# Branch projections in seven block products for two output tiles, with the weights' sums and parts made earlier and kept in DRAM

## The chip, the cores and the metric

The kernel runs on one core of one Trainium2 chip. The metric is device time in microseconds (us) of one execution. The time before is the median of three runs. Rows of the trace come from one profiled execution.

## The reference

One layer of a decoder: a normalized input, one input projection, three branches with gates, a projection of each branch, a merge by sigmoid gates, an output projection. Cut to what is computed around the change:

```python
mod = jax.nn.silu(c) @ w_ada + b_ada
shift, scale, gate = jnp.split(mod[:, None, :], 3, axis=-1)
h = _rmsnorm(x, norm_g) * (1 + scale) + shift
p = h @ w_in
a_b, a_c, a_h, a_g, b_u, b_v, b_g, c_x, c_g, m_a, m_b, m_c = jnp.split(p, IN_SPLITS, axis=-1)
...
merged = (jax.nn.sigmoid(m_a) * (y_a @ w_branch[0])
          + jax.nn.sigmoid(m_b) * (y_b @ w_branch[1])
          + jax.nn.sigmoid(m_c) * (y_c @ w_branch[2]))
x = x + gate * (merged @ w_out)
```

There are 1024 prompt positions and 8 samples, so T = 1032 columns, in two halves of H = 516 or four quarters of HC = 258. The model's width is 1024; `y_a`, `y_b`, `y_c` are 512 wide, so `w_branch` is three matrices of 512 x 1024. Everything is float32.

## The kernel before

Activations lie with features on partitions and positions on columns. A float32 product is made of three: each operand is split into a high part (a copy that rounds, on ScalarE) and a low part (a subtraction, on VectorE; both in `split`, L94 to L96), and TensorE forms high x high, high x low and low x high.

The stages, in order of time. **Head** (to about 30 us): x is loaded in eight tiles, ScalarE squares them, VectorE adds most squares (L206, L214), TensorE sums the rest over the partitions (`sum_squares`, `ss`, L190), then come the reciprocal root (`rm0x` and on), its spread over partitions (`spx` from `dgx`) and the modulation (`pada`). `warm_up` issues fill matmuls on a constant (`warm`, L308). **v stage** (30 to 88). **Input projection** (88 to 669): 28 pairs of output tiles, each by `pair_jobs` as seven block products of 24 matmuls of 258 columns in place of eight (Strassen's scheme). **Merge** (669 to 811): `merge_jobs` for the branches 1, 0, 2; for each of eight output tiles `wjob` issues 36 matmuls of 344 columns (four row blocks, three chunks, three parts) from one weight `p_...` and the branch output `yh`, `yl`, then VectorE multiplies by the gate `sig` (L1010, L1013) and adds to `acc` (L1014). **Output projection** (811 to 918).

From the projection on the work is a list of jobs. Each has a `dma`, a `split`, an `mm` and a `post`. `run_ahead` issues a job's `dma` and `split` so many us before its `mm` by the sum of the planned durations (`ahead`); `later` puts small tasks in a list that `do_behind` works off between jobs, up to 0.45 of a job's planned duration. All DMAs are issued on SyncE's queue in program order. Branch outputs and gates wait in DRAM (`y_d`, `sig_d`) and are loaded back in the merge. `gate_job` makes the products of the output gate (`pg`, `pgt`), between the branches of the merge.

## Time and profile before

| | |
|---|---|
| median of 3 runs | 922.15 us (920.43 to 922.79) |
| the profiled execution | 919.98 us, its span 918.2 us |
| TensorE busy | 906.0 us (99%), 6986 instructions |
| VectorE, ScalarE busy | 557.6 us (61%), 354.4 us (39%) |
| mean granted clock of TensorE | 0.993 |
| moved by DMA | 108.85 MB, 119 GB/s on the mean |

The profiled execution's own time is 1.78 us above its span. Busy shares are means over stages with different limits: which engine sets the pace is to be read stage by stage. In the rows below PE is TensorE, DVE is VectorE, ACT is ScalarE.

### The profile page before, as it was taken

Reading aid. Unit: us, or ns where it says so; the run is one execution under the profiler, and the core shown is the slowest. Engines: PE = TensorE matmul, PEld = TensorE weight load, DVE = VectorE, ACT = ScalarE, POOL = GpSimd, SP = SyncE. Lnnn points to the kernel's source line nnn. Section 1 sums busy time; section 2 is a strip of 40 time slices with the busy share of each in tenths; the row PEclk is TensorE's granted clock in tenths of the full one; section 3 lists DMA queues with packets and bytes.
Section 4 is the critical chain, followed back from the end, with each engine's and each line's share of the span. In section 5 each row is a group of like instructions: output and inputs, shape, how many; then the busy total and the mean of one; then the engine's idle time right before and its main releaser. Section 6 shows DMA issues by size and latency. Waiting matters only on the chain.

```text
span 918.2 us, 16664 instructions
## 1 busy us (share of the span) xinstructions
PE 906.0 (99%) x6986; PEld 880.3 (96%) x6986; DVE 557.6 (61%) x1006; ACT 354.4 (39%) x638; POOL 30.4 (3%) x72
## 2 busy tenths in 40 slices
PE   8999999999999999999999999999999999999996
PEld 8677999999999999999999999999999899999995
DVE  3786758566656666666475475674545366583635
ACT  5666472444332333335343444453522300421211
POOL 1450000000000000000000000000000000000001
PEclk9999999999999999999999999999999999999998
DMA  8805213113221212214204214142678834170103
GB/s 316 342 1 149 94 47 105 47 61 134 83 70 47 70 47 70 71 59 160 95 1 162 93 42 167 47 141 80 233 287 333 317 124 181 50 227 1 54 18 116
DMA packets 49627, 108.85 MB, mean 119 GB/s; under 512 B 10504, under 2 KB 21512, under 8 KB 49552
## 3 DMA queue, kind: packets, MB, share of 16 engines
q1 hardware_dynamic: 49552, 107.79, 33.8%
q8 instruction: 55, 0.90, 0.4%
q14 instruction: 20, 0.16, 0.1%
HBM read 83.93 MB, written 23.84 MB: 117 GB/s over the span
## 4 chain that ended last, share of the span: by engine, by line
PE 91%; DVE 1%; ACT 0%; DVEq 0%; issue 0%
PE o L1111 3%; PE o L1113 3%; PE o L1112 3%; PE g_2B L558 2%; PE g_2B L561 2%; PE g_2B L560 2%; PE g_1B L560 2%; PE g_1B L561 2%; PE g_0B L561 2%; PE g_0B L560 2%; PE g_3B L561 2%; PE g_3B L560 2%; PE g_0B L558 2%; PE g_3B L558 2%; PE g_1B L558 2%; PE u0B L558 1%
## 5 line engine op out<-in xcount | busy, mean ns | idle before, releaser
L1111 PE MATMUL o<-mh,woh 128*128 128x388 f32 (+1 forms) x192 | 62.0, 323 | 0.0
L1113 PE MATMUL o<-mh,wol 128*128 128x388 f32 (+1 forms) x192 | 61.3, 319 | 0.0
L1112 PE MATMUL o<-ml,woh 128*128 128x388 f32 (+1 forms) x192 | 61.3, 319 | 0.0
L1111 PEld LDWEIGHTS o<-mh,woh 128*128 128x128 f32 x192 | 36.1, 188 | 0.3
L1112 PEld LDWEIGHTS o<-ml,woh 128*128 128x128 f32 x192 | 36.1, 188 | 0.3
L1113 PEld LDWEIGHTS o<-mh,wol 128*128 128x128 f32 x192 | 36.1, 188 | 0.0
L1214 ACT ACTIVATE osq<-xr 128x388 f32<-128x388 f32 (+1 forms) x21 | 10.3, 491 | 48.1 <-DVE xr L1203 28.0
L360 PE MATMUL v<-bvw,hhi 128*128 128x512 f32 x64 | 26.4, 413 | 0.2 <-ACT hhi L277 0.2
L95 ACT ACTIVATE mh<-acc 128x516 fp32r<-128x516 f32 (+1 forms) x14 | 9.2, 688 | 44.9 <-DVE acc L1014 41.2
L362 PE MATMUL v<-bvw,hlo 128*128 128x512 f32 x64 | 25.5, 398 | 0.7 <-DVE hlo L281 0.7
L361 PE MATMUL v<-bvw,hhi 128*128 128x512 f32 x64 | 25.2, 394 | 0.0
L1200 DVE SCALAR_TENSOR_TENSOR xr<-o,gt,xr 128x384 f32<-128x384 f32 x16 | 9.8, 614 | 18.5 <-PE o L1113 18.5
L558 PE MATMUL g_2B<-t,g_2w 128*128 128x258 f32 x72 | 20.4, 283 | 0.0
L560 PE MATMUL g_1B<-hlo,g_1wB 128*128 128x258 f32 x72 | 20.4, 283 | 0.0
L561 PE MATMUL g_1B<-hhi,g_1wB 128*128 128x258 f32 x72 | 20.4, 283 | 0.0
L561 PE MATMUL g_0B<-hhi,g_0wB 128*128 128x258 f32 x72 | 20.4, 283 | 0.0
L561 PE MATMUL g_2B<-hhi,g_2wB 128*128 128x258 f32 x72 | 20.4, 283 | 0.0
L561 PE MATMUL g_3B<-hhi,g_3wB 128*128 128x258 f32 x72 | 20.3, 283 | 0.0
L560 PE MATMUL g_2B<-hlo,g_2wB 128*128 128x258 f32 x72 | 20.3, 283 | 0.0
L560 PE MATMUL g_1B<-t,g_1w 128*128 128x258 f32 x72 | 20.3, 283 | 0.0
L560 PE MATMUL g_3B<-hlo,g_3wB 128*128 128x258 f32 x72 | 20.3, 282 | 0.0
L560 PE MATMUL g_0B<-hlo,g_0wB 128*128 128x258 f32 x72 | 20.3, 282 | 0.0
(1043 smaller groups left out, 3481.0 us busy)
## 6 DMA issues: line engine op xcount, KB each, us to landing
sig<-sd SPq DMA_DIRECT2D x24, 516.0 KB, 6.4
ada<-in_ada SPq DMA_DIRECT2D x16, 512.0 KB, 8.9
yr<-yd SPq DMA_DIRECT2D x12, 516.0 KB, 9.9
x<-in_xT SPq DMA_DIRECT2D x16, 256.0 KB, 5.5
gr<-in_ada_g SPq DMA_DIRECT2D x8, 512.0 KB, 10.3
wor<-in_wo SPq DMA_DIRECT2D x8, 512.0 KB, 6.3
xr<-in_xf SPq DMA_DIRECT2D x8, 512.0 KB, 4.4
sd<-g_0o SPq DMA_DIRECT2D x6, 516.0 KB, 3.4
```

The costliest lines, as they stand in the source:

```text
L95: A_.activation(hi, src, AF.Copy)
L360: PE.matmul(vacc[i], lhsT=lh, rhs=w[:, 0, :], start=start, stop=False)
L361: PE.matmul(vacc[i], lhsT=lh, rhs=w[:, 1, :], start=False, stop=False)
L362: PE.matmul(vacc[i], lhsT=ll, rhs=w[:, 0, :], start=False, stop=stop)
L558: PE.matmul(o, lhsT=w[:, 0, f_], rhs=bh, start=start and k == 0, stop=False, skip_group_check=True)
L560: PE.matmul(o, lhsT=w[:, 0, f_], rhs=bl, start=False, stop=False, skip_group_check=True)
L561: PE.matmul(o, lhsT=w[:, 1, f_], rhs=bh, start=False, stop=stop and k == KW - 1, skip_group_check=True)
L1111: PE.matmul(o, lhsT=wo_h[k][:, w], rhs=cols(mhi[k]), start=start, stop=False)
L1112: PE.matmul(o, lhsT=wo_h[k][:, w], rhs=cols(mlo[k]), start=False, stop=False)
L1113: PE.matmul(o, lhsT=wo_l[k][:, w], rhs=cols(mhi[k]), start=False, stop=stop)
L1200: V.scalar_tensor_tensor(x[:, :m], ps[:, :m], gt[:, f, 0:1], x[:, :m], ALU.mult, ALU.add)
L1214: A_.activation(o_like(c, sq), x, AF.Square)
```

## The change

In the merge each pair of output tiles (12 pairs in all: three branches of four) is computed as a product of 2 x 2 blocks with seven block products P1 to P7 in place of eight. The left operand is a weight of 512 x 256, cut in four blocks `A11` to `A22` of 256 x 128; the right operand is the branch output, 512 rows and 1032 columns, cut in four blocks of 256 x 516. Each block product is 12 matmuls of 258 columns. P1, P6, P7 and P4 pile up in one pair of banks (`B1`), P5 and P3 in another (`B5`); a third (`B2`) starts as a copy of P1 that ScalarE makes (`seed`) and takes P2. ScalarE copies partial results out (`snap`), VectorE adds and multiplies them (`added`, `gated`).

The sums of weight blocks (`S1` to `S4`) and all high and low parts are made beside 12 of the projection pairs (`WP`), stored to DRAM (`w_d`) and loaded in the merge 16 us ahead. The sums of blocks of `y` (`T1` to `T4`) and their parts are made as `later` tasks, for the first branch beside the last two projection pairs, for the others beside the tiles of the branch before (`LAST`, `NEXT`). The gate's products move beside two projection pairs (`RG`). In the head VectorE adds one more square, TensorE sums half as many, and the fill matmuls stand elsewhere. After a job's `post` the list of tasks is worked off by `do_behind` with the job's `room` negated.

```diff
-FILL, FILL_O = 4, (3, 7)
+WP, WAT = (4, 5, 6, 7, 8, 10, 12, 13, 16, 19, 22, 25), 2
...
+RG = (9, 11)
...
+WD, SD = 16.0, 8.0
...
+NEXT = {(1, "P2"): "dma", (1, "P4"): "B11", (1, "P3"): "T1+", (2, "P5"): "T1", (2, "P2"): "B21 T3+", (2, "P6"): "T2+ T4+",
+        (3, "P5"): "T2 B22", (3, "P2"): "T3", (3, "P6"): "T4"}
...
+LAST = {(1, 2): "dma", (1, 4): "B11", (1, 5): "T1+", (1, 6): "T1", (0, 0): "B21", (0, 1): "T3+", (0, 2): "T2+", (0, 3): "T4+",
+        (0, 4): "T2", (0, 5): "B22", (0, 6): "T3", (0, 7): "T4"}
...
+FILL, FILL_O = (10, 1, 3), (3, 7)
...
-        for hf in (1, 0):
-            sums(sq[i - 2], hf, hf == 1, False)
+        warm_up(FILL[0])
         for hf in (1, 0):
             c = cols_of(hf)
-            V.tensor_tensor(sq[i][:, c], sq[i][:, c], sq[i - 1][:, c], ALU.add)
-            sums(sq[i], hf, False, True)
+            for j in (i - 1, i):
+                V.tensor_tensor(sq[j][:, c], sq[j][:, c], sq[j - 1][:, c], ALU.add)
+            sums(sq[i], hf, hf == 1, True)
+            warm_up(FILL[1] if hf else 0)
...
-    warm_up(FILL)
+    warm_up(FILL[2])
...
+            self.room = 0.45 * dur if room is None else room
...
+    def branch_weights(br, i):
+
+        st = {}
...
+            st["raw"] = S(f"wr{br}{i}", 4 * WB)
+            Q.dma_start(st["raw"], ins["wbr"][br, i])
...
+                if j == 0:
+                    V.tensor_tensor(s[0], a[2], a[3], ALU.add)
+                    V.tensor_tensor(s[1], s[0], a[0], ALU.subtract)
+                else:
+                    V.tensor_tensor(s[2], a[0], a[2], ALU.subtract)
+                    V.tensor_tensor(s[3], a[1], s[1], ALU.subtract)
...
+                n = len(WA[x]) * WB
+                hi, lo = S(f"wh{br}{i}{x}", n, F32R), S(f"wl{br}{i}{x}", n, F32R)
...
+                else:
+                    split(st.pop("s"), hi, lo)
+                for h, t in enumerate((hi, lo)):
+                    w_d[br, i, x, h] = dp.tile([P, n], F32, tag=f"wd{br}{i}{x}{h}", name=f"wd{br}{i}{x}{h}")
+                    Q.dma_start(w_d[br, i, x, h], f32(t))
...
+        def post():
+            later(0.7, sums(0))
+            later(0.7, sums(1))
+            later(1.2, parts("s"))
+            later(1.0, parts("a"))
+
+        Job(dma, post=post, ahead=(5.0, 0.0))
...
+            for b in ("B11", "B21", "B12", "B22"):
+                raw[b] = S3(f"yr{br}{b}", 2, H)
+                for j in range(KQ):
+                    Q.dma_start(raw[b][:, j, :], y_d[br, KQ * (b[1] == "2") + j][:, cols_of(int(b[2]) - 1)])
+
...
+        tasks = {b: split_block(b) for b in ("B11", "T1", "B21", "T2", "B22", "T3", "T4")}
+        tasks |= {"T1+": summed_block("T1", "B12", "B11", ALU.subtract),
+                  "T3+": summed_block("T3", "B22", "B12", ALU.subtract, "B12"),
+                  "T2+": summed_block("T2", "T3", "B11", ALU.add, "B11"),
+                  "T4+": summed_block("T4", "B21", "T2", ALU.subtract, "B21")}
...
+            def dma():
+                for x, names in WA.items():
+                    for h in range(2):
+                        t = st[x, h] = S(f"pw{br}{i}{x}{h}", len(names) * WB, F32R)
+                        Q.dma_start(f32(t), w_d[br, i, x, h])
...
+            def s_dma():
+                for m in (m0, m1):
+                    st[m] = S(f"sig{br}_{m}", T)
+                    Q.dma_start(st[m], sig_d[br, m])
...
+            def mm(bank, a, b, start, stop):
...
+                    while b not in blk:
+                        behind.pop(0)[1]()
+                    bh, bl = blk[b]
+                    for c in range(2):
+                        if start:
+                            st[bank, c] = PS(f"p{br}{i}{bank}{c}")
+                        o = st[bank, c][:, :HC]
+                        for k in range(KQ):
...
+                            PE.matmul(o, lhsT=st[x, 0][:, w], rhs=bh[:, k, cs[c]], start=start and k == 0, stop=False, **kw)
+                            PE.matmul(o, lhsT=st[x, 0][:, w], rhs=bl[:, k, cs[c]], start=False, stop=False, **kw)
+                            PE.matmul(o, lhsT=st[x, 1][:, w], rhs=bh[:, k, cs[c]], start=False,
+                                      stop=stop and k == KQ - 1, **kw)
...
+                def f():
...
+                    for c in range(2):
+                        A_.activation(st[to][:, cs[c]], st[bank, c][:, :HC], AF.Copy)
...
+            def seed():
+                for c in range(2):
+                    st["B2", c] = PS(f"p{br}{i}B2{c}")
+                    A_.activation(st["B2", c][:, :HC], st["B1", c][:, :HC], AF.Copy)
...
+            def gated(m, half, bank):
...
+                for c in range(2):
+                    V.tensor_tensor(s[:, at(half, c)], st.pop((bank, c))[:, :HC], s[:, at(half, c)], ALU.mult)
...
+            def added(m, bank, to, drop):
+                t = st.pop(to)
+                for c in range(2):
+                    V.tensor_tensor(t[:, cs[c]], st[bank, c][:, :HC], t[:, cs[c]], ALU.add)
+                    if drop:
+                        del st[bank, c]
+                V.tensor_tensor(st[m][:, H:], t, st[m][:, H:], ALU.mult)
...
+                    V.tensor_tensor(acc[m], acc[m], st.pop(m), ALU.add)
...
+            def right():
+                added(m0, "B5", "u2", True)
+
+            def last():
+                gated(m1, 0, "B1")
+                later(1.3, lambda: summed(m0))
+                later(1.3, lambda: summed(m1))
+
+            J = lambda x, f, d=None, r=RM, a=0.0: (lambda: Job(d, None, x, f, dur=1.45, ahead=(a, 0.0), room=r))
+            return {
+                "P1": J(mm("B1", "A11", "B11", True, False), seed, dma, a=WD),
+                "P5": J(mm("B5", "S1", "T1", True, False), snap("B5", "p5")),
+                "P2": J(mm("B2", "A12", "B21", False, True), lambda: gated(m0, 0, "B2"), s_dma, r=-1.0, a=SD),
+                "P6": J(mm("B1", "S2", "T2", False, False), snap("B1", "u2")),
+                "P3": J(mm("B5", "S4", "B22", False, True), right, r=0.0),
+                "P7": J(mm("B1", "S3", "T3", False, False), lambda: added(m1, "B1", "p5", False), r=0.0),
+                "P4": J(mm("B1", "A22", "T4", False, True), last, r=-1.0),
+            }
...
     for i, (args, after) in enumerate(pairs):
+        if i in WP:
+            after = {**(after or {}), WAT: lambda w=prepared.pop(0): branch_weights(*w)}
+        if i in RG:
+            after = {**(after or {}), **{x: gp.pop(0) for x in (2, 4)}}
...
         pair_jobs(*args, after=after, early_b21=i == 0)
...
-    merge_jobs(0, 1)
-    g2 = [gate_job(0)]
-    g2.append(gate_job(1))
-    merge_jobs(1, 0)
-    for f in g2:
-        f()
-    merge_jobs(2, 2)
+    hooks[0](LAST[0, 7])
+    flat = [(n, i, t) for n in range(3) for i, t in enumerate(branches[n])]
+
+    def go(j, x):
+        n, i, t = flat[j]
+        t[x]()
+        if n < 2 and (i, x) in NEXT:
+            hooks[n + 1](NEXT[i, x])
+
+    go(0, "P1")
+    for j in range(len(flat)):
+        for x in ("P5", "P2", "P6", "P3", "P7") if j + 1 < len(flat) else ("P5", "P6", "P3", "P7", "P2"):
+            go(j, x)
+        if j + 1 < len(flat):
+            go(j + 1, "P1")
+        go(j, "P4")
 
...
-        do_behind(0.45 * job.dur)
+        do_behind(job.room)
         if job.post:
             job.post()
+        do_behind(-job.room)
```

In the head, TensorE's first rows before the change. `warm` is a fill, `ss` a column sum, `pada` the modulation, `spx` the spread; x12 is a row's count.

```order
L308 MATMUL warm<-ones 128x128 x55
L190 MATMUL ss<-ones,sq_253 86x1 x12
L190 MATMUL ss<-ones,sq_272 86x1 x12
L289 MATMUL pada_310<-ada_0_181,sc 32x256 x4
L289 MATMUL pada_310<-ada_1_182,sc 32x256 x4
L308 MATMUL warm<-ones 128x128 x4
L239 MATMUL spx_334<-dgx_326,ones 128x258
L239 MATMUL spx_336<-dgx_326,ones 128x258
L300 MATMUL pada_310<-sel_84,adap_319 128x9 x2
```

And the same place after it:

```order
L323 MATMUL warm<-ones 128x128 x65
L204 MATMUL ss<-ones,sq_272 86x1 x6
L323 MATMUL warm<-ones 128x128
L204 MATMUL ss<-ones,sq_272 86x1 x6
L304 MATMUL pada_313<-ada_0_181,sc 32x256 x4
L304 MATMUL pada_313<-ada_1_182,sc 32x256 x4
L323 MATMUL warm<-ones 128x128 x3
L254 MATMUL spx_336<-dgx_328,ones 128x258
L254 MATMUL spx_338<-dgx_328,ones 128x258
```

The two groups of 12 sums became two of six; ten more fills stand ahead of the first, one between the two, and three instead of four ahead of the spread.

On TensorE, where the merge begins, one output tile before (name: branch 1, tile 0 of weight 0, chunk 0 to 2):

```order
L490 MATMUL p1_00p0_7682<-yh1_0_7596,p1_0h_7612 128x344
L490 MATMUL p1_00p1_7683<-yh1_0_7596,p1_0h_7612 128x344
L490 MATMUL p1_00p2_7684<-yh1_0_7596,p1_0h_7612 128x344
L492 MATMUL p1_00p0_7682<-yl1_0_7597,p1_0h_7612 128x344
L492 MATMUL p1_00p1_7683<-yl1_0_7597,p1_0h_7612 128x344
L492 MATMUL p1_00p2_7684<-yl1_0_7597,p1_0h_7612 128x344
L494 MATMUL p1_00p0_7682<-yh1_0_7596,p1_0l_7613 128x344
L494 MATMUL p1_00p1_7683<-yh1_0_7596,p1_0l_7613 128x344
L494 MATMUL p1_00p2_7684<-yh1_0_7596,p1_0l_7613 128x344
```

And after, the second half of P1 and the first of P5 (`p10B1` is the bank pair B1 of branch 1, pair 0; the digit behind it is the half; `pw10a` and `pw10s` are the reloaded weight blocks and weight sums, 0 the high and 1 the low part):

```order
L1120 MATMUL p10B11_8054<-yh1B11_7750,pw10a0_7866 128x258
L1121 MATMUL p10B11_8054<-yl1B11_7751,pw10a0_7866 128x258
L1122 MATMUL p10B11_8054<-yh1B11_7750,pw10a1_7868 128x258
L1120 MATMUL p10B11_8054<-yh1B11_7750,pw10a0_7866 128x258
L1121 MATMUL p10B11_8054<-yl1B11_7751,pw10a0_7866 128x258
L1122 MATMUL p10B11_8054<-yh1B11_7750,pw10a1_7868 128x258
L1120 MATMUL p10B50_8069<-yh1T1_7823,pw10s0_7870 128x258
L1121 MATMUL p10B50_8069<-yl1T1_7824,pw10s0_7870 128x258
L1122 MATMUL p10B50_8069<-yh1T1_7823,pw10s1_7872 128x258
L1120 MATMUL p10B50_8069<-yh1T1_7823,pw10s0_7870 128x258
```

Each bank gets six matmuls per product (12 for both) and there are seven such products for two output tiles, where there were 72 matmuls of 344 columns. The weights are no longer those split on the spot.

On VectorE, in the second branch (0), two output tiles before:

```order
L1013 TENSOR_TENSOR sig0_0_8000<-p0_00p0_8128,sig0_0_8000 128x344
L1013 TENSOR_TENSOR sig0_0_8000<-p0_00p1_8129,sig0_0_8000 128x344
L1013 TENSOR_TENSOR sig0_0_8000<-p0_00p2_8130,sig0_0_8000 128x344
L1014 TENSOR_TENSOR acc0_7721<-acc0_7721,sig0_0_8000 128x1032
L1013 TENSOR_TENSOR sig0_1_8047<-p0_01p0_8175,sig0_1_8047 128x344
L1013 TENSOR_TENSOR sig0_1_8047<-p0_01p1_8176,sig0_1_8047 128x344
L1013 TENSOR_TENSOR sig0_1_8047<-p0_01p2_8177,sig0_1_8047 128x344
L1014 TENSOR_TENSOR acc1_7768<-acc1_7768,sig0_1_8047 128x1032
```

And after, in the third pair of tiles of the same branch (L110 is the low part of a block of `y` for the third branch):

```order
L1145 TENSOR_TENSOR sig0_4_8772<-p02B20_8830,sig0_4_8772 128x258
L1145 TENSOR_TENSOR sig0_4_8772<-p02B21_8832,sig0_4_8772 128x258
L110 TENSOR_TENSOR yl2B11_8882<-yr2B11_8705,yh2B11_8881 128x1032
L110 TENSOR_TENSOR yl2T1_8898<-yr2T1_8828,yh2T1_8897 128x1032
L1150 TENSOR_TENSOR p02pu_8864<-p02B50_8849,p02pu_8864 128x258
L1150 TENSOR_TENSOR p02pu_8864<-p02B51_8856,p02pu_8864 128x258
L1153 TENSOR_TENSOR sig0_4_8772<-p02pu_8864,sig0_4_8772 128x516
L1150 TENSOR_TENSOR p02pu_8864<-p02B10_8814,p02pu_8864 128x258
L1150 TENSOR_TENSOR p02pu_8864<-p02B11_8821,p02pu_8864 128x258
L1153 TENSOR_TENSOR sig0_5_8774<-p02pu_8864,sig0_5_8774 128x516
L110 TENSOR_TENSOR yl2B21_8960<-yr2B21_8708,yh2B21_8959 128x1032
L1145 TENSOR_TENSOR sig0_5_8774<-p02B10_8814,sig0_5_8774 128x258
```

For one pair of tiles six reads of 344 columns gave way to eight of 258 and two products of 516, and low parts of the next branch's blocks stand between them.

On ScalarE, where the merge begins, after the change (`g2_3` is the last gate pair of the projection, `yh1T3` and `yh1T4` are high parts of blocks of the first branch):

```order
L988 ACTIVATE g2_3o2_7968<-g2_3B10_7797 128x258
L988 ACTIVATE g2_3o2_7968<-g2_3B11_7810 128x258
L989 ACTIVATE g2_3o2_7968<-g2_3o2_7968 128x516
L990 ACTIVATE g2_3o1_7937<-g2_3o1_7937 128x1032
L109 ACTIVATE yh1T3_8061<-yr1B12_7587 128x1032
L1140 ACTIVATE p10B20_8065<-p10B10_8047 128x258
L1140 ACTIVATE p10B21_8067<-p10B11_8054 128x258
L109 ACTIVATE yh1T4_8083<-yr1B21_7584 128x1032
L1134 ACTIVATE p10pu_8087<-p10B50_8069 128x258
L1134 ACTIVATE p10pu_8087<-p10B51_8076 128x258
```

The copies of P1 (L1140) stand behind the last gate's sigmoids and one high part; before the change the merge had no operation of ScalarE between two matmul groups on a bank.

## Rows read from the trace of the kernel before

**Rows 1.** The page's first lines: span, and busy time with its share and instructions.
```profile
span 918.2 us, 16664 instructions
...
PE 906.0 (99%) x6986; PEld 880.3 (96%) x6986; DVE 557.6 (61%) x1006; ACT 354.4 (39%) x638; POOL 30.4 (3%) x72
```

**Rows 2.** Stretches of the span: busy time (and count) by engine, granted clock, DMA share, GB/s.
```profile
core 0: us, PE busy (x) PEld busy (x) DVE busy (x) ACT busy (x) POOL busy (x), PEclk, DMA share, GB/s
...
164.00:404.00 240.00, 240.00 (x2004) 240.00 (x2003) 153.65 (x273) 87.10 (x183) 0.11 (x1) 1.00 0.22 71
669.00:715.00 46.00, 46.00 (x298) 45.49 (x300) 20.77 (x34) 10.38 (x11) 0.00 (x0) 1.00 0.85 313
680.00:690.00 10.00, 10.00 (x65) 10.00 (x64) 3.95 (x7) 2.12 (x2) 0.00 (x0) 1.00 1.03 411
750.00:760.00 10.00, 10.00 (x65) 10.00 (x64) 8.32 (x12) 0.00 (x0) 0.00 (x0) 1.00 0.62 209
```

**Rows 3.** The chain of waits at the merge's borders: start us, us, what.
```profile
669.19 0.47 PE p_00p L490 x3
...
714.49 3.57 PE pg L1039 x32
718.06 0.68 PE p_00p L490 x3
...
763.65 1.69 PE pgt L1048 x16
765.34 0.58 PE p_00p L490 x3
...
810.88 0.18 PE o L1111
```

**Rows 4.** Timeline of TensorE: first matmuls of two projection pairs (start us, us).
```profile
628.74 0.28 PE L558 MATMUL g_2B<-hhi,g_2wB 128*128 128x258 f32 x1
...
648.91 0.28 PE L558 MATMUL g_3B<-hhi,g_3wB 128*128 128x258 f32 x1
```

**Rows 5.** Timeline of VectorE, and a ScalarE group (xcount, busy us, mean ns).
```profile
599.22 0.75 DVE L580 TENSOR_TENSOR g_0o<-g_0B,g_0p 128x258 f32<-128x258 f32 x2
599.89 0.68 DVE L96 TENSOR_TENSOR g_0w<-g_0b,g_0w 128x512 fp32r<-128x512 f32 x1
...
748.88 4.66 DVE L96 TENSOR_TENSOR yl<-yr,yh 128x1032 fp32r<-128x1032 f32 x4
...
L570 ACT ACTIVATE g_2p<-g_2B 128x258 f32<-128x258 f32 x12 | 4.6, 386 | 6.8 <-PE g_2B L561 6.7
```

**Rows 6.** The head: timeline of TensorE, of VectorE, and two stretches as in rows 2.
```profile
16.75 5.39 PE L190 MATMUL ss<-ones,sq 128*86 128x1 f32 x48 [1.23 <-DVE sq L206]
22.07 1.93 PE L289 MATMUL pada<-ada,sc 128*32 128x256 f32 x16
23.93 1.90 PE L308 MATMUL warm<-ones 128*128 128x128 f32 x8
25.67 1.04 PE L239 MATMUL spx<-dgx,ones 86*128 86x258 f32 x4
...
27.96 1.07 PE L289 MATMUL pada<-ada,sc 128*32 128x256 f32 x16
29.27 0.50 PE L360 MATMUL v<-bvw,hhi 128*128 128x512 f32 x1 [0.25 <-ACT hhi L277]
...
17.52 1.30 DVE L214 TENSOR_TENSOR sq<-sq,sq 128x516 f32<-128x516 f32 x2 [0.93 <-ACT sq L209]
22.17 0.17 DVE L222 TENSOR_SCALAR rm0x<-ss 86x12 f32<-86x12 f32 x1 [3.35 <-PE ss L190]
...
23.54 1.44 DVE L231 TENSOR_TENSOR dgx<-ident,rm1x 86x258 f32<-86x258 f32 x4
...
18.00:20.00 2.00, 2.00 (x21) 2.00 (x20) 0.82 (x2) 0.02 (x1) 0.00 (x0) 0.67 1.01 374
22.00:24.00 2.00, 2.00 (x18) 0.71 (x18) 1.36 (x7) 0.27 (x1) 0.00 (x0) 0.50 1.02 389
```

**Rows 7.** Timeline of ScalarE where the merge begins.
```profile
669.23 0.39 ACT L971 ACTIVATE g_3o<-g_3B 128x258 f32<-128x258 f32 x1 [1.04 <-PE g_3B L561]
669.51 0.63 ACT L972 ACTIVATE g_3o<-g_3o 128x516 f32<-128x516 f32 x1
670.30 1.07 ACT L973 ACTIVATE g_3o<-g_3o 128x1032 f32<-128x1032 f32 x1 [0.16 <-DVE g_3o L580]
671.27 1.04 ACT L95 ACTIVATE p_1h<-p_1r 128x1024 fp32r<-128x1024 f32 x1
```

More of the change, by code (lines that the diff above doesn't have):

```diff
@@ L981, in merge_jobs @@
     def merge_jobs(n, br):
-        share = {}
-        ys = {}
+        raw, blk = {}, {}
         def y_dma():
-            do_behind()
-            for j in range(KW):
-                ys[j] = S(f"yr{br}_{j}", T)
-                Q.dma_start(ys[j], y_d[br, j])
-        def y_split():
-            for j in range(KW):
-                yhi[br, j] = S(f"yh{br}_{j}", T, F32R)
-                ylo[br, j] = S(f"yl{br}_{j}", T, F32R)
-                split(ys.pop(j), yhi[br, j], ylo[br, j])
-        Job(y_dma, y_split, ahead=(20.0, 8.0) if n == 0 else (40.0, 18.0))
@@ new lines, in summed_block, with f, split_block @@
+        def summed_block(b, x, y, op, new=None):
+            def f():
+                o = S3(f"yr{br}{b}", 2, H) if new is None else raw[new]
+                V.tensor_tensor(o, raw[x], raw[y], op)
+                if new:
+                    del raw[new]
+                raw[b] = o
+            return f
+        def split_block(b):
+            def f():
+                blk[b] = S3(f"yh{br}{b}", 2, H, F32R), S3(f"yl{br}{b}", 2, H, F32R)
+                split(raw[b], *blk[b])
+                if b not in ("B11", "B21"):
+                    del raw[b]
+            return f
@@ new lines, in merge_jobs, with hook @@
+        tasks = {b: split_block(b) for b in ("B11", "T1", "B21", "T2", "B22", "T3", "T4")}
[3 more added lines that the diff above has]
+                  "T4+": summed_block("T4", "B21", "T2", ALU.subtract, "B21")}
+        def hook(x):
+            if x == "dma":
+                Job(y_dma, ahead=(4.0, 0.0))
+            else:
+                Job(post=lambda: [later(1.2, tasks[t]) for t in x.split()])
@@ L1007, in post_p @@
                 if n == 0:
[L1008 to L1014 removed]
+                    acc[m] = st.pop(m)
+                else:
+                    V.tensor_tensor(acc[m], acc[m], st.pop(m), ALU.add)
@@ L1015, in post_p @@
                 if n == 2 and m < EARLY:
-                    split_merged(m)
-            if m % 2 == 0:
-                share = {}
-            Job(s_dma, ahead=(17.0, 0.0))
-            wjob(f"p{br}_{m // 2}", ins["wbr"][br, m // 2], 2, KW,
-                 lambda: ([yhi[br, j] for j in range(KW)], [ylo[br, j] for j in range(KW)]),
-                 post_p, share, m % 2, ahead=(18.0, 12.0))
+                    later(1.3, lambda: split_merged(m))
+            def right():
+                added(m0, "B5", "u2", True)
@@ L1026, in gate_job @@
+        return hook, [tiles(i) for i in range(KD // 2)]
     def gate_job(b):
@@ L1081, in hybrid_step_kernel @@
     pairs += [(x, None) for x in gates]
+    gp = [f for b in range(2) for f in gate_job(b)]
+    hooks, branches = zip(*(merge_jobs(n, br) for n, br in enumerate((1, 0, 2))))
+    prepared = [(br, i) for br in (1, 0, 2) for i in range(KD // 2)]
     for i, (args, after) in enumerate(pairs):
-        pair_jobs(*args, after=after, early_b21=i == 0)
-    merge_jobs(0, 1)
-    g2 = [gate_job(0)]
-    g2.append(gate_job(1))
-    merge_jobs(1, 0)
-    for f in g2:
-        f()
-    merge_jobs(2, 2)
+        if i in WP:
+            after = {**(after or {}), WAT: lambda w=prepared.pop(0): branch_weights(*w)}
+        if i in RG:
+            after = {**(after or {}), **{x: gp.pop(0) for x in (2, 4)}}
+        first = {x: lambda b=b: hooks[0](b) for (e, x), b in LAST.items() if i == len(pairs) - 1 - e and x < 7}
+        after = {**(after or {}), **first}
+        pair_jobs(*args, after=after, early_b21=i == 0)
+    hooks[0](LAST[0, 7])
[12 more added lines that the diff above has]
+        go(j, "P4")
     wo_h, wo_l, xr, oacc = {}, {}, {}, {}
```

58 lines of the change are left out of this document (42 added, 16 removed).

## The prediction

> **What bounds the kernel now.** I read the page first. TensorE is busy for 906.0 of 918.2 us [rows 1], so only fewer or cheaper matmuls, or an earlier start of the dense stretch, can shorten the kernel. Next, the table of stretches: between 164 and 404 us (projection) TensorE is busy for 240.00 of 240.00 us at the full granted clock, and from 669 to 715 (first branch of the merge) for 46.00 of 46.00, with VectorE at 20.77 and ScalarE at 10.38 [rows 2]. No wait can be saved there; the count and size of the matmuls are the price. Then the chain of waits for the borders of the merge: 669.19, the gate products at 714.49, the second branch at 718.06, the gate's transposes at 763.65, the third branch (765.34, since the transposes take 1.69), and the output projection at 810.88 [rows 3]. Last the head, where the clock is half or two thirds of full [rows 6].
>
> **The matmuls.** The three branches take 714.49 - 669.19 = 45.30, 763.65 - 718.06 = 45.59 and 810.88 - 765.34 = 45.54 us [rows 3], together 136.43 us for 864 matmuls of 344 columns: 0.1579 each. The new ones have 258 columns. The projection runs just that shape in the same block scheme: from the first matmul of one pair (628.74) to that of the next (648.91) are 20.17 us for 168 of them [rows 4], 0.1201 each. The change needs 3 branches x 4 tiles x 7 products x 12 = 1008, so 121.0 us. **Gain: 15.4 us.** The price per column is then 0.465 ns against 0.459 before, so the smaller matmul loses almost nothing. The gate products (3.57 and 1.69 us in [rows 3]) are only moved, from the merge into two projection pairs: neither gain nor loss on TensorE.
>
> **The head.** Before, VectorE makes the last two half-width adds at 17.52 (1.30 for two), yet the column sums, 24 matmuls shown as 48 records, run from 16.75 for 5.39 us, and the mean is taken at 22.17. While those one-column matmuls run, the granted clock falls: 0.67 in 18 to 20 us, 0.50 in 22 to 24. The products of the modulation then take 1.93 us (1.07 for the same 16 records at 27.96), and the four fill matmuls behind them 1.90 us, so the spread begins at 25.67, though its operand is made from 23.54 on [rows 6]. After, there are 12 sums, since VectorE adds the last three squares: four half-width adds of 0.65 in place of two. The first needs no square of the last load and can run when VectorE falls idle, at 17.52 - 0.93 = 16.59, up to 17.3; the other three from 17.52 to about 19.4. Ten fills stand ahead of the sums and one between the halves, so TensorE multiplies until about 17.8 rather than waiting from 15.5 on. The last six sums (12 records of 5.39 / 48 = 0.11) end near 20.5 with the start of the first of them, and the mean moves from 22.17 to about 20.5. From the mean to the operand of the spread is 23.54 - 22.17 = 1.37, plus about 0.7 for its half. If the clock stays up, the modulation's 1.07 and three fills (about 0.2 each at full clock) end before that, at 22.2, and the spread begins at 22.5 in place of 25.67: 3.2 us gained. If the clock falls as before, 1.93 and three fills at 0.475 end at 24.0: 1.6 gained. I take **3.0**, since the fills bridge the stretch in which the clock fell, and keep 1.6 for the range. That the rest of the head moves along rests on loads that already run at a share of 1.01 and 1.02 [rows 6], which cannot be hastened; the first products of the v stage start at 29.27, and a load that just arrived in time there would eat part of it.
>
> **Behind the matmuls: VectorE and ScalarE.** Prices: two reads of 258 columns from PSUM take 599.89 - 599.22 = 0.67 us of VectorE, an operation of 1032 columns 4.66 / 4 = 1.165 in a row of four; ScalarE takes 0.386 to read 258 columns [rows 5]. For 516 columns I put 0.61, on the line between the two. Each new tile has eight 258-column operations on VectorE and two of 516 (2.68 + 1.22 = 3.9 us), two accumulations of 1032 in the second and third branch (2.33), and in some tiles up to three sums or low parts of the next branch's blocks (3.5): 9.7 us in the fullest four tiles (the last two of the second branch, the first two of the third), 5 to 9 in the others, against 84 x 0.1201 = 10.1 us of TensorE. So VectorE stays below TensorE, barely. In the order of VectorE above, two 1032-column low parts stand ahead of the four adds that free a bank for the product P4; those adds can be late by one product (1.45 us, the next tile's P1 that was put between) before TensorE feels it. Two operations late together are 2.33, so up to 0.9 us may show in such a tile. From both sides: 0 and 4 x 0.9; I take **+0.6**, nearer to nothing, since at 750 to 760 VectorE was busy for 8.32 of 10 us and TensorE for all of them [rows 2].
>
> The first tile is different. Its P2 needs ScalarE to copy P1's bank (seed). In ScalarE's order the seed stands behind the last gate's sigmoids and one 1032-column high part. Before, that queue read 669.23, 669.51, 670.30 and the next began at 671.27 [rows 7]; with the high part (0.97 start to start) the seed begins at 672.24 and its first half ends at 672.6, while TensorE would reach P2 at 669.0 + 2 x 1.44 = 671.9. **+0.7.** In the last tile no next P1 is there to cover the add between P7 and P4; P2 stands there instead, and splits for the output projection lie ahead of the adds on VectorE: one operation of 1.165 and the pair, against 1.45 of cover. **+0.4** (0 to 1.2).
>
> **Beside the projection.** Twelve weights are summed and split there: each four sums of 256 columns and the parts of 1024, 512 and 256 columns, by the prices above about 3.5 us on VectorE and 1.8 on ScalarE, with 0.5 MB read and 1.8 MB written. Twelve of 28 pairs carry one. VectorE had 153.65 of 240 us [rows 2], 12.9 of a 20.17 us pair, so 16.4 of 20.17 with a weight; by my count of its operations the fullest pair comes to about 17.4. Nothing, then, though the cover is thin: where a pair's own low parts come late by more than the 6 us at which they are made ahead, TensorE would wait. The room for such tasks is 0.45 of a product as before, which spreads them. **0** (0 to 1.5).
>
> **The reloads.** A tile now reads 1.8 MB of parts and 1.06 MB of sigmoids, and a branch 2.1 MB of blocks: 3.4 MB per 10.1 us, 340 GB/s, where 680 to 690 shows 411 GB/s moved with TensorE untouched [rows 2]. Parts are asked for 16 us ahead and sigmoids 8 us ahead. **0** (0 to 4).
>
> **Sum:** -15.4 - 3.0 + 0.7 + 0.4 + 0.6 = -16.7 us. The profiled execution took 919.98 (1.78 outside its span), so 903.3 by it. That run lies 2.2 us below the median of 922.15, and 0.45 below the lowest of the three; from the median it would be 905.5. I predict the middle, **904.4**.
>
> **Rivals.**
> (a) *VectorE becomes the bound.* For: 9.7 of 10.1 us in four tiles, and single operations last longer than their pitch. If a read of 258 columns costs its whole 0.75 - 0.335 = 0.415 each time, a full tile takes 10.3 us, nothing is caught up from one to the next, and the 0.9 of above shows in each of the four with a rest in their neighbours: 4 us in place of 0.6, so about 908. Against: 8.32 of 10 us left no trace on TensorE.
> The Trainium skill, TensorEngine Tiling (Array Packing), section PSUM Bottleneck, says that tiling speeds up TensorE but not the emptying of PSUM, so that the copies may become the bottleneck. By it the merge would follow the PSUM reads, which rise from 24 x 1032 = 24,768 to 12 x 14 x 258 = 43,344 columns; the time it gives is that of this rival.
> (b) *The clock falls in the head all the same.* Of 3.0 us 1.4 are lost: 905.8. For: one-column sums are still there, and 0.50 was granted as late as 22 to 24.
> (c) *A reload or a block comes late* in the merge, behind the sums stored and the sigmoids on the one queue: one wait of 3 to 5 us, 908.5. Against: the bytes fit, and the loads' buffers come free a tile before they are needed.
> (d) *The other side: every tile hands over with a wait.* P2 waits for the seed and P4 for the adds after P7, each behind an engine's queue, in all twelve tiles. The gain of 15.4 + 3.0 - 1.1 us is used up at 17.3 / 12 = 1.44 us per tile, and the kernel is slower by 0.3% (2.8 us) from 1.7 on, at 925. The seed alone is 0.386 after P1 with one product of 1.45 as cover, so it would need a 1032-column operation ahead of it in each tile; the order above shows that only in the first.
>
> **Chances.** The forecast 0.55; (a) 0.18; (b) 0.13; (c) 0.11; (d) 0.03. The low end: all small losses nothing and 15.8 of matmuls, 919.98 - 15.8 - 3.2 = 901.0. The high end takes (a) and (c): 910. Range 900.8 to 910. A difference of 0.3% or 2.8 us is what a measurement here can tell from none; only (d) or several mishaps together reach it: faster 0.95, same 0.02, slower 0.03.
>
> **What would show it.** TensorE records rise by about 140 (144 more products, 24 fewer records of sums, some more fills). A branch should last 40.3 us, plus the named waits. The spread should begin at 22.5 with a granted clock of 1.00 in 20 to 24; 24 with 0.5 would be (b). VectorE's idle time in the four full tiles near nothing together with TensorE waits in front of P4 would be (a). Waits on the parts or the blocks as releasers would be (c). I would be wrong if 258-column matmuls cost more than 0.120 here, with other weights loaded per matmul than in the projection, or if the prepared weights made TensorE wait in the projection.

## The result, and the profile after

The changed kernel takes 905.43 us (median of 4 runs, 904.50 to 906.72) against 922.47 (median of 4, 920.43 to 922.90): ratio 0.982, 95% interval 0.9805 to 0.9836, 17.0 us less. The forecast was 904.4, in a range of 900.8 to 910. The profiled execution took 906.72 with a span of 905.0, so it stands 1.3 us above its median, while that of before stood 2.5 below its own. The two spans differ by only 13.2; the missing 3.8 us lies in the head, which differs from one execution to the next (see the part on the head below).

The page's first lines, after:

```profile
span 905.0 us, 17515 instructions
...
PE 890.9 (98%) x7126; PEld 864.2 (95%) x7126; DVE 625.0 (69%) x1149; ACT 398.5 (44%) x743; POOL 30.4 (3%) x72
```

TensorE has 15.1 us less work in 140 more records; VectorE has 67 us more [rows 1].

Timeline of TensorE at the merge's borders and at its two waits (start us, us; the bracket is idle time and what ended it):

```profile
674.71 0.28 PE L578 MATMUL g_3B<-t,g_3w 128*128 128x258 f32 x1
674.83 0.28 PE L1120 MATMUL p10B<-yh1B,pw10a 128*128 128x258 f32 x1
...
677.57 0.28 PE L1122 MATMUL p10B<-yh1T,pw10s 128*128 128x258 f32 x1
678.17 0.39 PE L1120 MATMUL p10B<-yh1B,pw10a 128*128 128x258 f32 x1 [0.33 <-ACT p10B L1140]
678.40 0.30 PE L1121 MATMUL p10B<-yl1B,pw10a 128*128 128x258 f32 x1
...
794.75 0.28 PE L1122 MATMUL p23B<-yh2B,pw23a 128*128 128x258 f32 x1
795.56 0.39 PE L1120 MATMUL p23B<-yh2T,pw23a 128*128 128x258 f32 x1 [0.53 <-DVE p23pu L1150]
795.79 0.28 PE L1121 MATMUL p23B<-yl2T,pw23a 128*128 128x258 f32 x1
...
797.11 0.34 PE L1287 MATMUL o<-mh,woh 128*128 128x388 f32 x1
```

The merge runs from 674.83 to 797.11, 122.28 us, where before it took 141.69 with the gate's products in it [rows 3]. The list of what TensorE waited for from 86 us to the end (us in total, times, longest) has only two entries:

```profile
engine line waited for: us in total, times, longest us
PE p23B L1120 <- DVE p23pu L1150: 0.5, 1, 0.5
PE p10B L1120 <- ACT p10B L1140: 0.3, 1, 0.3
```

Stretches of the merge in which VectorE is full (columns as in [rows 2]):

```profile
744.00:754.00 10.00, 10.00 (x85) 10.00 (x85) 9.81 (x15) 3.26 (x7) 0.00 (x0) 1.00 0.88 291
754.00:764.00 10.00, 10.00 (x86) 10.00 (x85) 9.91 (x16) 5.89 (x10) 0.00 (x0) 1.00 1.00 386
764.00:774.00 10.00, 10.00 (x86) 10.00 (x85) 9.81 (x16) 4.19 (x8) 0.00 (x0) 1.00 0.99 380
```

VectorE is busy for 9.81 to 9.91 of 10 us in three stretches on end, and TensorE for all of them. The DMA engines, at a share of 0.88 to 1.00, stopped nothing either.

The head, timeline of TensorE, then two stretches:

```profile
14.73 3.07 PE L323 MATMUL warm<-ones 128*128 128x128 f32 x26
20.04 1.05 PE L204 MATMUL ss<-ones,sq 128*86 128x1 f32 x12 [2.25 <-DVE sq L228]
...
21.36 1.16 PE L204 MATMUL ss<-ones,sq 128*86 128x1 f32 x12
22.45 1.93 PE L304 MATMUL pada<-ada,sc 128*32 128x256 f32 x16
24.31 1.55 PE L323 MATMUL warm<-ones 128*128 128x128 f32 x6
25.70 1.04 PE L254 MATMUL spx<-dgx,ones 86*128 86x258 f32 x4
...
29.30 0.50 PE L375 MATMUL v<-bvw,hhi 128*128 128x512 f32 x1 [0.25 <-ACT hhi L292]
```

```profile
18.00:20.00 2.00, 0.00 (x0) 0.00 (x0) 1.50 (x3) 1.41 (x3) 0.00 (x0) 1.00 1.04 417
...
22.00:24.00 2.00, 2.00 (x22) 1.03 (x21) 0.97 (x6) 0.27 (x1) 0.00 (x0) 0.55 1.04 423
```

These answer to [rows 6]. The last tiles of x landed later in this execution (ScalarE begins the last squares at 18.54 us, before the change at 16.86), TensorE stood for 2.25 us ahead of the sums, and the granted clock, which was at its upper level (1.00) up to 22 us, was at its lower one (0.50) for most of the next two, 0.55 on the mean, while the sums and the modulation ran. So the v stage begins at 29.30, where it did before (29.27).

Where the time went between the two profiled executions, from the timelines (start of the stage, us; the chain in [rows 3] has the merge's borders 0.16 later, at 669.19 and 810.88):

| | v stage | projection | merge | output projection | span |
|---|---|---|---|---|---|
| before | 29.27 | 88.02 | 669.03 | 810.72 | 918.2 |
| after | 29.30 | 88.05 | 674.83 | 797.11 | 905.0 |

The head gives nothing here. The projection is 5.77 us longer; the gate's products, 5.26 us in [rows 3], were moved into it. The merge is 19.41 shorter, and the stretch from the output projection to the end 0.4 longer (107.5, 107.9). Together that is -19.41 + 5.77 + 0.4 = -13.2 us, all of it outside the head.

### The profile page after: what moved, and what is told of

Same layout as the page of the kernel before. It is cut to its first block, busy times and chain, and to the rows that moved or that the text cites. A ratio compares the mean times of both kernels' runs of the same rounds, so it can differ in the third digit from the quotient of the medians.

```text
span 905.0 us, 17515 instructions
## 1 busy us (share of the span) xinstructions
PE 890.9 (98%) x7126; PEld 864.2 (95%) x7126; DVE 625.0 (69%) x1149; ACT 398.5 (44%) x743; POOL 30.4 (3%) x72
## 4 chain that ended last, share of the span: by engine, by line
PE 90%; DVE 1%; ACT 1%; issue 0%; DVEq 0%
PE o L1287 3%; PE o L1288 3%; PE o L1289 3%; PE g_2B L575 2%; PE g_1B L577 2%; PE g_2B L577 2%; PE g_0B L577 2%; PE g_3B L577 2%; PE g_0B L578 2%; PE g_2B L578 2%; PE g_1B L575 2%; PE g_0B L575 2%; PE g_1B L578 2%; PE g_3B L578 2%; PE g_3B L575 2%; PE u0B L575 1%
## 5 line engine op out<-in xcount | busy, mean ns | idle before, releaser
L323 PE MATMUL warm<-ones 128*128 128x128 f32 x158 | 21.4, 300 | 1.1 <-DVE ones L130 1.1
L323 PEld LDWEIGHTS warm<-ones 128*128 128x128 f32 x158 | 20.6, 214 | 1.9 <-DVE ones L130 1.1
L575 PE MATMUL g_1B<-hhi,g_1wB 128*128 128x258 f32 x72 | 20.4, 283 | 0.0
L575 PE MATMUL g_2B<-hhi,g_2wB 128*128 128x258 f32 x72 | 20.4, 283 | 0.0
L578 PE MATMUL g_1B<-hhi,g_1wB 128*128 128x258 f32 x72 | 20.4, 283 | 0.0
L578 PE MATMUL g_2B<-hhi,g_2wB 128*128 128x258 f32 x72 | 20.3, 283 | 0.0
```

Source lines behind the costliest of these rows:

```text
L323: PE.matmul(ps[:, :P], lhsT=ones, rhs=ones, start=True, stop=True)
L575: PE.matmul(o, lhsT=w[:, 0, f_], rhs=bh, start=start and k == 0, stop=False, skip_group_check=True)
L578: PE.matmul(o, lhsT=w[:, 1, f_], rhs=bh, start=False, stop=stop and k == KW - 1, skip_group_check=True)
```

## The experiments

Medians and ratios are against runs of the kernel before on the same chip; three groups of four kernels shared such runs (medians 920.52, 920.66 and 922.02).

**head_alone**: the kernel before with only the new head (`FILL` and `sum_squares` as in the change's diff, nothing else).

> The kernel before with nothing but the new head: one more square added on VectorE, 12 column sums in place of 24, fills 10, 1, 3. Theory A (as predicted): the spread begins near 22.5 us in place of 25.67 and the granted clock stays at 1.00 between 20 and 24 whenever the tiles of x land at the times of the run before (last square near 17); the median falls by 2 to 3 us, ratio 0.997 to 0.998. Theory B (the fills don't hold the clock): the clock falls to 0.5 to 0.6 in 22 to 26 in nearly every execution, the spread stays at 25.7, and the ratio is 0.999 to 1.000.

Measured: 919.76 against 920.52, ratio 0.9991 (0.9977 to 1.0005). Timeline of TensorE, and one stretch:

```profile
18.99 1.05 PE L190 MATMUL ss<-ones,sq 128*86 128x1 f32 x12 [0.47 <-DVE sq L214]
...
21.31 1.07 PE L290 MATMUL pada<-ada,sc 128*32 128x256 f32 x16
...
23.35 1.11 PE L240 MATMUL spx<-dgx,ones 86*128 86x258 f32 x4
...
27.03 0.50 PE L361 MATMUL v<-bvw,hhi 128*128 128x512 f32 x1 [0.25 <-ACT hhi L278]
```

```profile
22.00:24.00 2.00, 1.90 (x17) 1.37 (x10) 1.86 (x8) 0.90 (x2) 0.00 (x0) 1.00 1.03 417
```

Here TensorE stood for 0.47 us, the clock stayed at 1.00, the spread began at 23.35 and the v stage at 27.03, 2.24 us ahead of before. The projection began at 86.94, only 1.08 ahead. The list of TensorE's waits in between shows where most of the rest goes:

```profile
PE v L363 <- DVE hlo L282: 1.1, 2, 0.5
PE v L361 <- ACT hhi L278: 0.5, 2, 0.2
```

`hlo` is VectorE's, `hhi` ScalarE's; before, two waits for `hlo` took 0.7 us and one for `hhi` 0.2. In this execution theory A's mechanism is there; the ratio is theory B's: 0.8 us on the median, with an interval that ends at 2.1. The mean granted clock of each run on record suggests why: it is 0.997 here, 0.996 to 0.998 in three more of the twelve runs, and 0.989 to 0.995 in the other eight. In the profiles with the new head it is 0.997 to 0.998 where the clock stayed up in the head and 0.994 to 0.995 where it fell, so by this mark (an estimate) it fell in eight of twelve.

**head_undone**: the changed kernel with the old head.

```diff
-FILL, FILL_O = (10, 1, 3), (3, 7)
+FILL, FILL_O = 4, (3, 7)
...
-        warm_up(FILL[0])
+        for hf in (1, 0):
+            sums(sq[i - 2], hf, hf == 1, False)
...
```

> The changed kernel with the head of before. Theory A: 2 to 3 us above the changed kernel, so a ratio to the kernel before near 0.985 where the changed kernel has 0.982. Theory B: the same ratio as the changed kernel within 0.001. In either, the merge lasts 122.3 us from its first matmul to the output projection, as in the changed kernel's profile.

Measured: 908.98, ratio 0.9879 (0.9862 to 0.9896), 3.7 us above the changed kernel beside it (after_again), so more than theory A's 2 to 3. One stretch of its profile:

```profile
24.00:34.00 10.00, 10.00 (x47) 6.85 (x40) 5.67 (x15) 5.17 (x12) 1.86 (x6) 0.50 1.03 407
```

The clock stayed at its lower level through all of this stretch, and the v stage began at 32.63. The old head has worse draws than the one in [rows 6]. The merge lasted 122.28 us, as expected.

**more_fills**: 18 and 4 fills for 10 and 1.

```diff
-FILL, FILL_O = (10, 1, 3), (3, 7)
+FILL, FILL_O = (18, 4, 3), (3, 7)
```

> The changed kernel with 18 fills ahead of the sums and 4 between the halves (10 and 1 before), nothing else. In the changed kernel's profile the last tiles of x landed about 1.6 us later than in the profile of before, TensorE stood idle for 2.25 us ahead of the sums, and the clock fell behind that. Theory A: more fills bridge that gap, the granted clock stays at 1.00 up to 26 us, the spread begins at 23 to 23.5 even with late tiles, and at 22.8 to 23 with early ones (the extra fills then cost some tenths); median 0 to 1 us below the changed kernel. Theory B: the clock falls all the same, the spread begins at 26 or later, and the time is equal or up to 1 us above.

Measured: 905.51 (905.18 to 906.19), ratio 0.9840 (0.9826 to 0.9854). No idle time ahead of the sums, clock 1.00, spread at 23.94, v stage at 27.62, projection at 86.92. The mechanism is theory A's, though the spread is later than its 23.5; the median is that of the changed kernel (0.2 above it). In the profiled execution part of the gain went into a wait in the projection, which no other profile has. TensorE's list of waits has the first line below, VectorE's timeline the second:

```profile
PE bg1B L575 <- DVE bg1o L607: 0.5, 1, 0.5
211.48 0.42 DVE L1017 TENSOR_TENSOR ws<-wr 128x256 f32<-128x256 f32 x1 [1.81 <-DMA wr<-in_wbr]
```

VectorE stood for 1.81 us until a raw weight (`wr`) had landed; the weight's sums and parts followed, ahead of an add (`bg1o`) of the pair itself. TensorE waited for that add, and the projection lasts 587.40 us where it lasts 586.7 to 586.8 in the other profiles.

**after_again**: the changed kernel, unedited.

> The changed kernel once more, beside the others on one chip, for their differences: ratio 0.982, as measured. Its profile is a second draw of the head. Theory A: if the tiles of x land early in it, the spread begins near 22.5 and the clock stays at 1.00 in 20 to 24; Theory B: the clock falls in 22 to 26 whatever the landing times.

Measured: 905.29 (903.94 to 905.93), ratio 0.9837 (0.9822 to 0.9852). Idle 1.10 us ahead of the sums, clock 0.89 in 20 to 22 and 0.50 in 22 to 24, v stage at 27.90: the tiles of x landed as early as in [rows 6], and still the clock fell. That is against theory A's plain form, in which landing alone decides.

**no_cover**: the next tile's P1 behind P4.

```diff
-        if j + 1 < len(flat):
-            go(j + 1, "P1")
         go(j, "P4")
+        if j + 1 < len(flat):
+            go(j + 1, "P1")
```

> The changed kernel with each next tile's P1 put behind P4, no longer between P7 and P4 (the seed then has P5 alone ahead of P2, as before). Theory A (as predicted): the cover carries the hand-over; without it P4 waits for the adds after P7 in every tile, about 0.5 us as in the last tile of the changed kernel, and up to 2 us in the four tiles in which VectorE is full: 5 to 12 us in all over eleven tiles, ratio to the kernel before 0.988 to 0.996. Theory B: VectorE is early enough in any order, and the time stays within 1 us of the changed kernel.

Measured: 911.05, ratio 0.9888 (0.9867 to 0.9909); the merge lasts 127.69 us, 5.41 more than with the cover. The first of eleven new waits, in the timeline of TensorE:

```profile
683.51 0.28 PE L1122 MATMUL p10B<-yh1T,pw10s 128*128 128x258 f32 x1
684.01 0.39 PE L1120 MATMUL p10B<-yh1T,pw10a 128*128 128x258 f32 x1 [0.23 <-DVE p10pu L1150]
684.24 0.29 PE L1121 MATMUL p10B<-yl1T,pw10a 128*128 128x258 f32 x1
```

All eleven are alike (0.20 to 0.25 idle, from the first tile to the last but one), as much in light tiles as in full ones, so the price is the add itself and not VectorE's load: theory A at its low end, and its 2 us in the full tiles wrong.

**dve_one**: one more operation of VectorE per tile.

```diff
+                if m % 2 == 0:
+                    V.tensor_tensor(acc[m], acc[m], acc[m], ALU.max)
```

> The changed kernel with one more operation of 1032 columns on VectorE per tile (the larger of an accumulator and itself, which changes no value), behind the accumulation. Theory A: in the four full tiles VectorE, busy for 9.8 to 9.9 of 10 us, has nothing left; there the added 1.17 us each shows on TensorE, less one product's cover of 1.45 us that is used up once: 2 to 4 us more than the changed kernel. Theory B: VectorE's full tiles are followed by lighter ones and its list of tasks shifts freely: within 1 us of the changed kernel, with no TensorE wait on VectorE beyond those there.

Measured: 909.53, ratio 0.9878 (0.9853 to 0.9903), 4.2 us above the changed kernel's 905.29 (after_again, another group); the merge of its profile lasts 126.94 us, 4.66 more than without the operation. TensorE's waits from 86 us on:

```profile
PE p23B L1120 <- DVE p23pu L1150: 1.5, 1, 1.5
PE p21B L1120 <- ACT p21pu L1134: 1.4, 1, 1.4
PE p03B L1120 <- DVE p03pu L1150: 0.9, 1, 0.9
PE p10B L1120 <- ACT p10B L1140: 0.3, 1, 0.3
```

Twelve operations of 1.17 us are 14 us; three waits of 0.9 to 1.5 us came out, two in full tiles (p03, p21) and one in the last, which had 0.5 before. Two more matmuls (in p02 and p21) start 0.42 and 0.40 us after the one ahead of them, where 0.12 is usual; the list does not show them. The wait on ScalarE (p21) is VectorE's too: the copy `p21pu` stood behind a high part (`mh`) that had waited 3.9 us for the added operation itself (L1161 of that kernel). Theory A, a little above its 2 to 4 us: VectorE has less than one operation per tile to give there.

**late_loads**: reloads asked for later.

```diff
-WD, SD = 16.0, 8.0
+WD, SD = 5.0, 5.0
```

> The changed kernel with the reloaded weights asked for 5 us ahead instead of 16 and the gates 5 instead of 8. Theory A: the reloads' lead is what keeps them off the path; 1.8 MB at about 400 GB/s take 4.6 us alone and share the queues with the gates and blocks of y, so P1 or P5 waits 1 to 4 us in most tiles: 10 to 40 us more. Theory B: the loads land in 5 us or less even so, and the time stays within 1 us of the changed kernel.

Measured: 911.5, ratio 0.9902 (0.9877 to 0.9926); the merge lasts 128.13 us. New entries among TensorE's waits:

```profile
PE p11B L1120 <- DMA pw11a<-wd11a: 1.6, 1, 1.6
PE p12B L1120 <- DMA pw12a<-wd12a: 0.9, 1, 0.9
...
PE p11B L1122 <- DMA pw11a<-wd11a: 0.4, 1, 0.4
PE p12B L1122 <- DMA pw12a<-wd12a: 0.4, 1, 0.4
```

The lead matters, but for two tiles and 5.9 us, not for most tiles and 10 to 40: theory A too high. And not all of the 5.9 us are waits. Counted from start to start, the four lose 4.35 us. Behind the first two, which stand in one tile, the granted clock fell to its lower level:

```profile
687.50:690.50 3.00, 3.00 (x16) 3.00 (x15) 0.56 (x2) 0.37 (x1) 0.00 (x0) 0.50 1.02 414
```

From 687.34 to 690.72 us matmuls of 258 columns start up to 0.22 us apart where 0.12 is usual, which costs 1.5 us more. Behind the other two waits the clock stayed at 1.00.

**tidy**: the two waits of the changed kernel taken away.

```diff
-                "P1": J(mm("B1", "A11", "B11", True, False), seed, dma, a=WD),
+                "P1": J(mm("B1", "A11", "B11", True, False), seed, dma, r=-1.0 if n == i == 0 else RM, a=WD),
...
-        Job(dma, spl, mm, post, dur=4.3, ahead=(16.0, 9.5))
+        Job(dma, spl, mm, post, dur=4.3, ahead=(16.0, 5.5 if k == 1 else 9.5))
```

> The changed kernel with two small moves: in the first tile the high part of a block of y goes behind the copies of P1 in ScalarE's order, and the split of the output projection's second weight begins 4 us later, behind the last tile's adds. Expected: the waits of 0.3 us (P2 for the copy) and 0.5 us (P4 for the add) vanish from TensorE's list, 0.5 to 0.8 us less than the changed kernel, hardly visible in the median; if other work takes the place ahead of the copy or the add, one or both waits stay.

Measured: 903.06, ratio 0.9807 (0.9785 to 0.9829). TensorE waits for nothing from 86 us to the end of the output projection's matmuls, and the merge takes 120.91 us (672.70 to 793.61), 1.37 less than in the changed kernel, where 0.5 to 0.8 was expected (the last section tells why). ScalarE's timeline at the first tile shows the move, the copies of P1 (L1140) ahead of both high parts:

```profile
674.66 0.65 ACT L1140 ACTIVATE p10B<-p10B 128x258 f32<-128x258 f32 x2
675.23 2.01 ACT L109 ACTIVATE yh1T<-yr1B 128x1032 fp32r<-128x1032 f32 x2
```

**tidy_2**: the same kernel again.

> The tidied kernel once more, beside the others on one chip: ratio 0.981 to 0.982, 1 to 2 us below the changed kernel's ratio of 0.982 to 0.984; a TensorE without any wait from the projection to the end of the output projection, and 120.9 us for the merge.

Measured: 903.33, ratio 0.9796 (0.9774 to 0.9818), a little below what was expected; a merge of 120.91 us without a wait.

**tidy_old_head** and **head_undone_2**: the old head (as in head_undone) in the tidied and, again, in the changed kernel.

> The tidied kernel with the head of before. Theory A: 1 to 2 us above the tidied kernel beside it. Theory B: 3 to 4 us above. The merge lasts 120.9 us from its first matmul to the output projection in either, as in the tidied kernel.

> The changed kernel with the head of before, a second time: the first gave 0.9879 where the changed kernel beside it had 0.9837, 3.9 us apart, though the new head alone saved only 0.8 us in the kernel before. Theory A (the head is worth 1 to 2 us, and the first profile, half clock up to about 34 us, was an unlucky draw): ratio 0.985 to 0.986, and a spread that begins between 25.5 and 26.5. Theory B (the old head costs more in the changed kernel): 0.988 again.

Measured: tidy_old_head 906.68, ratio 0.9827 (0.9803 to 0.9851), 3.35 above tidy_2; v stage at 31.44. head_undone_2 908.06, ratio 0.9843 (0.9820 to 0.9866); v stage at 29.66, spread at 25.96. The first is theory B's. The second has a ratio below either theory's and a spread within theory A's times; but it lies 4.73 us above tidy_2, its neighbour, and without the 1.37 us of waits that tidy_2 lacks that is 3.36, again theory B's distance.

**tidy_fills**: the tidied kernel with 14 and 2 fills.

> The tidied kernel with 14 fills ahead of the sums and 2 between the halves (10 and 1). If the idle time ahead of the sums is what lets the clock fall, the clock stays at 1.00 from 20 to 26 us in its profile also when a tile of x is late, and the time is 0 to 1 us below the tidied kernel, with a narrower spread; if the clock falls nevertheless, equal within 0.5 us.

Measured: 904.19, ratio 0.9813 (0.9790 to 0.9836). Timeline of TensorE and one stretch:

```profile
19.30 1.01 PE L204 MATMUL ss<-ones,sq 128*86 128x1 f32 x12
...
21.64 1.07 PE L304 MATMUL pada<-ada,sc 128*32 128x256 f32 x16
...
23.69 1.11 PE L254 MATMUL spx<-dgx,ones 86*128 86x258 f32 x4
...
27.36 0.50 PE L375 MATMUL v<-bvw,hhi 128*128 128x512 f32 x1 [0.25 <-ACT hhi L292]
```

```profile
22.00:24.00 2.00, 1.89 (x24) 1.20 (x16) 1.61 (x7) 1.12 (x3) 0.00 (x0) 1.00 1.02 415
```

The clock held in this execution, and the time did not fall below the tidied kernel's (0.9 us above tidy_2). Nor is the spread narrower: 903.95 to 906.71, against 901.69 to 904.54 in tidy_2. In the run of 906.71 the mean granted clock was 0.991, against 0.996 to 0.998 in the other three, so there it seems to have fallen all the same.

## Why the prediction was right, step by step

**Matmuls: right.** With no wait left (tidy) 1008 matmuls take 120.91 us, 0.1199 each, against 121.0 forecast; the gain is 136.43 - 120.91 = 15.5 (forecast 15.4). The price of a shape, read where the same kernel already runs it, held.

**Small waits: near in sum (1.37 us, forecast 1.7), wrong in one term.** First and last tile together cost 122.28 - 120.91 = 1.37 us, 0.59 and 0.80 from start to start (forecast 0.7 and 0.4). Taking away the two causes that were named took away the two waits and all of this. The 0.6 for VectorE's lag was not there: busy for 9.9 of 10 us, it was in time. Rival (a), and with it the rule of the Trainium skill, TensorEngine Tiling (Array Packing), section PSUM Bottleneck, that after a fourfold speed-up of TensorE the copies out of PSUM may become the bottleneck, did not come true here: no wait of TensorE in the full tiles stands in the trace. VectorE as a whole was close to its limit, as dve_one shows with one operation more per tile and a merge 4.66 us longer; but by the prediction's prices its reads of PSUM are only 8 x 0.335 = 2.7 of the 9.9 us.

**The other side (d): priced by no_cover.** Without the interleaved P1 each hand-over costs 5.41 / 11 = 0.49 us, a third of the 1.44 per tile that would have used up the gain.

**Beside the projection: right in eleven of twelve.** In the profiles of eleven runs with the new merge the prepared weights cost TensorE nothing: no wait stands in its list, and the projection lasts 586.7 to 586.8 us, against 581.0 before. In the twelfth, more_fills, the late weight cost 0.66 us: the cover was as thin as the prediction said, and one of its own signs of being wrong did show, within the range given (0 to 1.5). The 5.8 us are the gate's products, which cost 0.2 more than where they stood. Timeline of TensorE in the changed kernel, at the first of four places:

```profile
289.11 0.28 PE L578 MATMUL ag1B<-t,ag1w 128*128 128x258 f32 x1
289.31 1.92 PE L1198 MATMUL pg<-gr,sc 128*32 128x512 f32 x16
291.17 0.39 PE L575 MATMUL ag1B<-hhi,ag1wB 128*128 128x258 f32 x1
```

From 289.11 to 291.17 are 2.06 us where 0.12 is usual, and the next start is late as well. Before, they cost 5.26 in [rows 3] and 0.32 more in the products behind them (0.68 and 0.58 for 0.47 each), 5.58 in two places; now they cost 5.77 in four. "Neither gain nor loss" was so far wrong, and 0.3 of the 15.5 us above are theirs. The 0.4 us after the merge (0.2 in the tidied kernels) are spread over the stretch, 0.24 of them over the 384 matmuls of 388 columns, with no new wait among them; their cause was not found.

**Reloads: right** with the lead as given; a lead of 5 us costs 5.9 (rival c), 1.5 of them by the clock behind the first wait.

**The head: right in size by luck, wrong in how often its mechanism works.** Eight profiled executions with the new head (10, 1 and 3 fills), by the idle time ahead of the sums:

| idle ahead of the sums, us | 0.47 | 0.64 | 0.94 | 1.10 | 1.65 | 1.67 | 1.87 | 2.25 |
|---|---|---|---|---|---|---|---|---|
| granted clock, 22 to 24 us | 1.00 | 1.00 | 1.00 | 0.50 | 0.57 | 0.61 | 0.50 | 0.55 |
| v stage begins | 27.03 | 26.59 | 27.21 | 27.90 | 28.80 | 28.90 | 28.64 | 29.30 |
| projection begins | 86.94 | 85.94 | 85.98 | 87.30 | 87.53 | 87.66 | 87.41 | 88.05 |

(head_alone, dve_one, tidy, after_again, tidy_2, no_cover, late_loads, after.) The forecast, a clock that stays up, came true in three of eight; in five it was rival (b). The spread never began at 22.5 as forecast: at 22.91 to 23.54 in the three, at 23.64 to 25.70 in the five. The projection began at 88.02 in the execution of [rows 6], so a gain of 3.0 meant 85.0; the mean of the eight is 87.10, a gain of 0.9 on that execution. But the old head gave 91.99, 89.04 and 90.74 in three others, 89.95 on the mean of the four, and 2.85 us lie between the two means. So the new head came out later than forecast, and the old head's draw in [rows 6] was better than its mean; that the two misses cancel is luck. In pairs of one group the medians differ by 3.7 and 3.35.

The spans on record give an estimate over all runs. From the start of the projection to the end, the profiled executions of one merge agree within 0.1 us: 830.2 (before, head_alone), 816.9 (after, after_again, head_undone, head_undone_2), 815.3 (the four tidied ones). A run's span less this figure is the start of its projection. In the new merge it began at 89.5 on the mean with the old head (13 runs) and at 86.4 with the new one (17 runs of after, after_again, tidy and tidy_2), 3.1 apart. In the old merge it began at 88.8 (the 17 runs of the kernel before beside head_alone) and 87.8 (12 of head_alone), 1.1 apart. So the missing 3.8 us between the profiled executions is the old head's luck and the new one's lack of it.

What stays open is why head_alone saved only 0.8 us (at most 2.1). Its v stage took 59.91 us in the profile, where the others take 58.7 to 59.6, but one profile is no mean; and the kernel before alone began its projection at 88.8, 89.2 and 90.1 on the means of the three groups, so the groups themselves differ by 1.3 us. That an earlier v stage gives time back is not shown: that of tidy began at 27.21 and took 58.77 us, as before (58.75); that of head_undone_2 began at 29.66 and took 59.38. More fills held the clock in their profiles and gained nothing: more_fills lost 0.66 us in the projection, and the v stage of tidy_fills took 59.57.

**The sum.** Without the head the forecast was -15.4 + 1.7 = -13.7 us and the trace gives -13.2; with the head it was -16.7, and the medians differ by 17.0. From the median before, the sum gave 905.5, and 905.43 was measured; the forecast took about 1 us off because the profiled execution lay below the median, and that was the old head's good draw. The high end of the range is not what its sentence says: (a) and (c) at their own prices come to 904.4 + 3.6 + 4.1 = 912.1, not 910. No run of the changed kernel reached either.

## What to carry to other kernels

A product with an eighth fewer multiplications pays in full only if every hand-over between its products has a product of other work beside it: place the next tile's first product there, and price the hand-over by taking it out again. Here VectorE at 98 to 99% beside a full TensorE cost nothing, and one more operation per tile cost 4.7 us, so count operations per tile before adding any. A load that comes late can cost more than its wait: in late_loads a quarter of the loss was the lower clock behind it. Before a gain is read from two profiles, look at several draws of the stage in question: here the start of the projection moved by 2.1 us over eight profiles with one head and by 4.0 over four with the other.
